# A hybrid attention step on one core: the instruction order from a simulated timeline

## The chip, the cores and the metric

The kernel runs on one core of a Trainium2 chip. The metric is device time in microseconds for one execution; several executions are timed and their median is taken. One further execution is run under the hardware profiler, and the profile lines below come from it.

## The reference, cut to what matters

One layer of a streaming encoder is computed for 1024 new frames of a prompt and for 8 running streams of 16 frames each with 1024 past frames. The input projection (2048 x 8192) yields queries, keys, values and gates of two head groups; the stick-breaking heads and the retention heads are computed; an output projection (2048 x 2048) follows. Everything is float32.

```python
p = jnp.einsum('btd,de->bte', rms_norm(x), w_in)          # q,k,v,gate of 8 stick-breaking + 8 retention heads
# stick-breaking: strictly causal, no softmax
z = einsum(q, k) * HEAD_DIM ** -0.5
log_keep = where(strict, log_sigmoid(-z), 0.0)
later = cumsum(log_keep, reverse=True) - log_keep
a = where(strict, exp(log_sigmoid(z) + later), 0.0);  o_sb = einsum(a, v)
# retention: chunks with a decaying state
o_r = einsum(einsum(q, k) * intra, v) + einsum(q, s) * decay_read
s = s * exp(lg * n) + einsum(k, decay_write, v)
y = concat(head_rms_norm(o_sb) * silu(gate_sb), head_rms_norm(o_r) * silu(gate_r))
x = x + rms_norm(einsum('bte,ed->btd', y, w_out))
```

## The kernel before, in words

The frames are cut into nine tiles of 128 rows: eight of the prompt (0 to 7) and one that holds the 8 streams x 16 frames (`SAMPLE`). They are worked in two groups. The first has tiles 0 to 3 and the sample tile (640 columns, in pieces of 256 and 384), the second tiles 4 to 7 (512 columns). For each group the normalized input stands in SBUF as a high and a low part (`mov`), and the kernel goes through eight heads. A head has six projections written as `project` (L206, 128 x 128 weights moving over the group's columns) and, for every two heads, two written as `project_rows` (L252, for the values). Every float32 product is three matmuls of high and low parts. Weights come through `load_w`: a load on SP's queue (L192), a high part by ScalarE (`split`, L127) and a low part by VectorE (L128), in four buffers each; a buffer holds four 128 x 128 blocks.

The attention itself is done in side jobs. A job is a Python generator; `project` and `project_rows` call `tick()` after each small set of matmuls, and a tick lets one due job trace its next step. A job's `yield n` says after how many ticks its next step is due (the `D_...` constants). This fixes the program order, in which the steps of the jobs lie between the matmuls of the projections. The jobs of a head are:

- `retention` with `ret_branch`: a transpose of the keys through HBM (`s_rk`, read back into `ro`, transposed by VectorE at L765), scores (L668), products into the bank `pa` (L686), new state (L701).
- `stick_breaking` with `sb_branch`: scores `z` (L535), sigmoids, a scan, a transpose of the weights through HBM (`s_be`), the last step of the transpose on VectorE (L525), products into `pa` (L559), copied out (L562).
- `decode`, in the first group: cached keys `kc` are loaded by POOL (L585), transposed by VectorE into `kcT` (L610), multiplied (L601); after the scan and a round trip through HBM (`s_bd`, L635) the weights multiply the cached values `vc` (loaded at L616, used at L648); the result is copied from `pa` at L654 and L656. Its first instruction is `qp` (L569).
- `finish`: head normalization, a transpose through HBM (`s_o`), the product with the gate, a store to `s_y`.

The bank `pa` exists once, the score bank `z` three times, the projection's accumulators twice. After the second group's last head the output projection runs in panels of 512 columns (`out_panel`, L879 and L889 to L891), for three groups of tiles.

Nothing in the text sets the order on an engine beyond this program order. Leaving the `TileContext` runs a list scheduler: it keeps the program order as priority, simulates the machine, and at each simulated moment gives an engine the ready instruction of the highest priority; buffers are given out in the same pass. The order in which it does this is the order of each engine's instruction list. Semaphore waits are then put in; on the chip every engine works through its list in order. In the kernel before, the simulation charges each instruction one duration.

## Time and profile before

| what | value |
|---|---|
| median of 3 runs | 2477.28 us (2473.57 to 2478.8) |
| profiled execution | 2463.17 us, of which the span from the first to the last instruction is 2461.1 us |
| granted TensorE clock | 0.988 |
| busy: TensorE, VectorE, ScalarE, POOL | 2367.9, 1250.0, 903.8, 641.9 us |
| DMA | 418.65 MB, mean 170 GB/s |

PE is TensorE's matmuls, PEld its weight loads, DVE VectorE, ACT ScalarE; SPq and the like are an engine's own queue of instructions such as DMA issues. A line of waits reads: engine, tile and line, what it waited for, the total us, how many times, the longest.

### The profile page before, as it was taken

How to read it: one execution, taken by the hardware profiler on the slowest of the kernel's cores; microseconds unless marked ns; L12 is line 12 of the kernel's file. 1: busy time of each engine (PE TensorE's matmuls, PEld its weight loads, DVE VectorE, ACT ScalarE, POOL GpSimd, SP SyncE). 2: the span in 40 equal slices, each digit the busy share in tenths (PEclk: the TensorE clock that was granted, in tenths of full speed). 3: DMA queues.
4: the chain of work that ended last, by engine and by line, in shares of the span. 5: the costliest groups of instructions: out<-in, count | busy, mean ns of one | idle time of the engine just before them, and what ended most of it. 6: DMA issues, size and time to landing. Idle time of an engine off the chain costs nothing.

```text
span 2461.1 us, 40322 instructions
## 1 busy us (share of the span) xinstructions
PE 2367.9 (96%) x14832; PEld 2099.4 (85%) x14832; DVE 1250.0 (51%) x2362; ACT 903.8 (37%) x1913; POOL 641.9 (26%) x1029
## 2 busy tenths in 40 slices
PE   7999899999999999998799999999999998999998
PEld 7999888989898888988578898889889886878787
DVE  8245454454444454444545544554564555564544
ACT  6323232333233232233334434344344443444333
POOL 3244354443433344333402111120220211000000
PEclk9999999999999999999999999999999998999999
DMA  7769677695948678495955655665564566665553
GB/s 241 165 144 210 143 191 173 173 199 140 212 125 221 149 177 178 130 226 146 209 161 150 153 152 142 144 163 135 153 160 128 152 152 170 224 221 191 184 184 133
DMA packets 673094, 418.65 MB, mean 170 GB/s; under 512 B 223744, under 2 KB 617984, under 8 KB 670464
## 3 DMA queue, kind: packets, MB, share of 16 engines
q1 hardware_dynamic: 523760, 285.99, 45.9%
q0 software_dynamic: 32256, 71.36, 12.5%
q10 hardware_dynamic: 116880, 58.74, 8.6%
q8 instruction: 116, 1.90, 0.3%
q14 instruction: 82, 0.67, 0.1%
HBM read 336.24 MB, written 79.69 MB: 169 GB/s over the span
## 4 chain that ended last, share of the span: by engine, by line
PE 75%; DMA 10%; issue 9%; DVE 4%; POOL 1%; ACT 1%; SPq 0%; ACTq 0%; DVEq 0%; POOLq 0%
PE acc L206 38%; PE accn L252 14%; PE a L890 4%; PE a L891 4%; PE a L889 4%; PE pa L559 2%; DMA vc<-cache_sb_v 2%; PE z L535 2%; DMA wr<-w_in 1%; PE zc L601 1%; DMA ro<-s_rk 1%; DMA kc<-cache_sb_k 1%; DMA s_rk<-rk 1%; PE pa L648 1%; DMA s_be<-be 1%
## 5 line engine op out<-in xcount | busy, mean ns | idle before, releaser
L206 PE MATMUL acc<-ml,wh 128*128 128x256 f32 (+2 forms) x2304 | 677.0, 343 | 0.2 <-DVE ml L128 0.2
L206 PE MATMUL acc<-mh,wh 128*128 128x256 f32 (+2 forms) x2304 | 670.5, 341 | 6.5 <-ACT rv L262 3.8
L206 PE MATMUL acc<-mh,wl 128*128 128x256 f32 (+2 forms) x2304 | 669.9, 341 | 3.7 <-DVE wl L128 3.7
L128 DVE TENSOR_TENSOR wl<-wr,wh 128x512 fp32r<-128x512 f32 (+1 forms) x576 | 394.7, 691 | 503.5 <-ACT wh L127 498.5
L127 ACT ACTIVATE wh<-wr 128x512 fp32r<-128x512 f32 (+1 forms) x576 | 356.6, 625 | 730.4 <-PE acc L206 367.9
L206 PEld LDWEIGHTS acc<-mh,wh 128*128 128x128 f32 x2304 | 425.3, 189 | 51.3 <-issue 14.3
L206 PEld LDWEIGHTS acc<-mh,wl 128*128 128x128 f32 x2304 | 425.1, 189 | 47.6 <-issue 12.2
L206 PEld LDWEIGHTS acc<-ml,wh 128*128 128x128 f32 x2304 | 422.5, 190 | 40.3 <-issue 12.4
L585 POOL DMA_DIRECT2D kc<-cache_sb_k x512 | 331.4, 653 | 367.8 <-DVE kcT L610 167.5
L252 PE MATMUL accn<-whn,mh 128*128 128x256 f32 x1152 | 332.5, 289 | 0.0
L252 PE MATMUL accn<-wln,mh 128*128 128x256 f32 x1152 | 326.9, 284 | 3.8 <-DVE wln L128 3.8
L252 PE MATMUL accn<-whn,ml 128*128 128x256 f32 x1152 | 326.5, 284 | 0.0
L252 PEld LDWEIGHTS accn<-whn,mh 128*128 128x128 f32 x1152 | 221.2, 192 | 12.9 <-issue 10.8
L890 PE MATMUL a<-wl,mh 128*128 128x512 f32 (+1 forms) x576 | 221.2, 384 | 7.7 <-DVE wl L128 7.7
L252 PEld LDWEIGHTS accn<-wln,mh 128*128 128x128 f32 x1152 | 221.3, 192 | 7.0 <-DVE wln L128 5.5
L252 PEld LDWEIGHTS accn<-whn,ml 128*128 128x128 f32 x1152 | 221.0, 192 | 1.7 <-issue 1.7
L891 PE MATMUL a<-wh,ml 128*128 128x512 f32 (+1 forms) x576 | 220.5, 383 | 0.0
L889 PE MATMUL a<-wh,mh 128*128 128x512 f32 (+1 forms) x576 | 219.3, 383 | 1.0 <-DVE sg L279 0.6
L890 PEld LDWEIGHTS a<-wl,mh 128*128 128x128 f32 x576 | 109.3, 190 | 31.3 <-DVE wl L128 10.6
L127 ACT ACTIVATE whn<-wrn 128x512 fp32r<-128x512 f32 x128 | 79.8, 634 | 151.2 <-PE acc L206 39.8
L441 POOL DMA_DIRECT2D be<-s_be x128 | 94.1, 741 | 142.4 <-DMA s_be<-be 124.0
L128 DVE TENSOR_TENSOR wln<-wrn,whn 128x512 fp32r<-128x512 f32 x128 | 86.8, 687 | 83.4 <-ACT whn L127 82.8
(184 smaller groups left out, 2602.4 us busy)
## 6 DMA issues: line engine op xcount, KB each, us to landing
wr<-w_in SPq DMA_DIRECT2D x384, 256.0 KB, 3.8
wr<-w_out SPq DMA_DIRECT2D x184, 256.0 KB, 3.6
wrn<-w_in SPq DMA_DIRECT2D x128, 256.0 KB, 3.1
kc<-cache_sb_k POOLq DMA_DIRECT2D x512, 64.0 KB, 4.3
vc<-cache_sb_v SPq DMA_DIRECT2D x64, 512.0 KB, 8.7
xt<-x_prompt SPq DMA_DIRECT2D x8, 1024.0 KB, 6.1
xr<-x_prompt SPq DMA_DIRECT2D x8, 1024.0 KB, 6.0
out<-out ACTq DMA_DIRECT2D x12, 512.0 KB, 2.9
```

Source lines behind the costliest of these rows:

```text
L127: nc.scalar.activation(hi, src, AF.Copy)
L128: nc.vector.tensor_tensor(lo, src, hi.bitcast(F32), ALU.subtract)
L206: last = nc.tensor.matmul(a[:, :m], lhs[:, j, :], rhs[w][:, j, o : o + m], start=(w == 0 and j == 0 and n == 0), stop=(w == KT // WQ - 1 a ...
L252: nc.tensor.matmul(a, lhs[q][:, jj, ts], rhs[:, j, :], start=(w == 0 and j == 0 and n == 0 and t % 2 == 0), stop=(w == KT // 2 - 1 and j = ...
L441: q.dma_start(raw[32 * i : 32 * i + 32, :].rearrange("p (k a) -> p k a", a=32), s[:, :, 32 * i : 32 * i + 32].rearrange("k (j b) a -> b (k ...
L535: nc.tensor.matmul(z[:, :c], q2[a][:, i * P : (i + 1) * P], k2[b][:, s : s + c], start=(m == 0), stop=(m == 2),)
L559: nc.tensor.matmul(po[:, :P], at[:, j, :], vn[:, j, :], start=(j == 0), stop=(j == t))
L585: nc.gpsimd.dma_start(kc[32 * i : 32 * i + 32, :].rearrange("p (k d) -> p k d", d=32), cache_k[0, 2 * c + j, s * 512 : (s + 1) * 512, h, 3 ...
L601: nc.tensor.matmul(z[r, :], qp[:, j, r], ready[c // 2][:, c % 2, :], start=(j == 0), stop=(j == 1))
L889: nc.tensor.matmul(a[:, :width], hi[q][:, j, ts], wh, start=(k == 0), stop=False)
L890: nc.tensor.matmul(a[:, :width], hi[q][:, j, ts], wl, start=False, stop=False)
L891: nc.tensor.matmul(a[:, :width], lo[q][:, j, ts], wh, start=False, stop=(k == KT - 1))
```

## The change

The context is told to build the order against a simulated timeline: instructions hold sequencers, queues and engines there, and transfers share the DMA engines, in place of one duration for each instruction. The kernel's text, its program order, its tiles and its buffers are the same.

```diff
-    with tile.TileContext(nc) as tc:
+    with tile.TileContext(nc, schedule_with_timeline_sim=True) as tc:
         tile_hybrid_step(tc, *args)
```

## Prediction

> **What bounds the kernel now.** I read the page first (busy shares and chain), then a table by stage, then TensorE's own waits, and then one stall instruction by instruction.
>
> ```profile
> span 2461.1 us, 40322 instructions
> PE 2367.9 (96%) x14832; PEld 2099.4 (85%) x14832; DVE 1250.0 (51%) x2362; ACT 903.8 (37%) x1913; POOL 641.9 (26%) x1029
> PE 75%; DMA 10%; issue 9%; DVE 4%; POOL 1%; ACT 1%; SPq 0%; ACTq 0%; DVEq 0%; POOLq 0%
> ```
>
> TensorE is busy for 2367.9 of 2461.1 us, so 93.2 us are idle in all, and that is nearly the most that a new order can give. The number of matmuls stays. The other engines have half their time free or more.
>
> ```profile
> core 0: us, PE busy (x) PEld busy (x) DVE busy (x) ACT busy (x) POOL busy (x), PEclk, DMA share, GB/s
> 0.00:42.00 42.00, 26.65 (x194) 25.70 (x195) 31.10 (x79) 26.95 (x44) 19.76 (x30) 0.96 0.83 274
> 42.00:1205.00 1163.00, 1123.83 (x8075) 1026.62 (x8075) 558.61 (x1132) 375.03 (x821) 454.11 (x757) 0.99 0.75 173
> 1205.00:1240.00 35.00, 25.80 (x187) 24.82 (x187) 17.97 (x25) 8.76 (x16) 6.92 (x11) 0.85 0.87 203
> 1240.00:1985.00 745.00, 744.18 (x4264) 648.28 (x4264) 392.46 (x687) 295.88 (x609) 126.37 (x196) 1.00 0.59 150
> 1985.00:2110.00 125.00, 112.12 (x511) 91.89 (x509) 67.10 (x123) 52.96 (x116) 18.34 (x28) 0.95 0.62 162
> 2110.00:2461.00 351.00, 335.31 (x1608) 282.11 (x1608) 182.80 (x319) 144.22 (x309) 16.44 (x7) 0.99 0.57 190
> ```
>
> These are the start, the eight heads of the first group (with the decode jobs), the hand-over between the groups, the second group, its end under the first output panel, and the output panels. The second group has 0.8 us of idle TensorE in 745: no order can better it, only spoil it. The first group has 39.2 us, the hand-over 9.2, the end 12.9. So what there is to win lies where side jobs run tightest. TensorE's waits say which:
>
> ```profile
> PE pa L559 <- DVE so L656: 12.2, 4, 7.5
> PE p0t L338 <- DVE dg L355: 10.5, 1, 10.5
> PE pa L559 <- DVE kp L525: 9.8, 4, 4.8
> PE pa L648 <- DMA vc<-cache_sb_v: 9.8, 5, 4.0
> PE a L890 <- DVE wl L128: 7.7, 7, 1.6
> PE rs L668 <- DVE rk L290: 5.1, 1, 5.1
> PE zc L601 <- DVE kcT L610: 3.9, 4, 1.6
> ...
> PE pa L641 <- DVE kp L635: 2.1, 2, 1.1
> ...
> PE zc L601 <- DVE kb L454: 1.0, 1, 1.0
> PE pSs L739 <- DVE st L742: 0.8, 1, 0.8
> ```
>
> (Total us, times, longest.) The small matmuls of the side jobs account for 12.2 + 9.8 + 9.8 + 5.1 + 3.9 + 2.1 + 1.0 + 0.8 = 44.7 us. The start (10.5) and the weights of the output panels (7.7) are apart. The longest, 7.5 us, shows what kind of fault it is. First two pieces of the chain of waits, then VectorE, then TensorE:
>
> ```profile
> 1092.49 7.66 DMA s_rk<-rk
> ...
> 1104.39 9.75 DMA ro<-s_rk
> ```
>
> ```profile
> 1107.07 0.71 DVE L610 STREAM_TRANSPOSE kcT<-kc 128x512 f32<-128x512 f32 x1 [5.05 <-DMA kc<-cache_sb_k]
> 1114.26 0.84 DVE L765 STREAM_TRANSPOSE rkn<-ro 128x640 f32<-128x640 f32 x1 [6.48 <-DMA ro<-s_rk]
> ...
> 1116.59 0.28 DVE L654 COPY so<-pa 128x128 f32<-128x128 f32 x1
> ...
> 1117.65 0.34 DVE L656 SCALAR_TENSOR_TENSOR so<-pa,dec,so 128x128 f32<-128x128 f32 x1
> ```
>
> ```profile
> 1118.14 1.62 PE L559 MATMUL pa<-vn,kb 128*128 128x128 f32 x6 [7.47 <-DVE so L656]
> ```
>
> VectorE stands at a transpose whose operand makes a round trip through HBM; the two transfers took 7.66 and 9.75 us. Behind it in the same queue stands the copy that would free the only `pa` bank, and TensorE waits for that bank. The list was built as if the round trip were shorter than it is.
>
> **The change, part by part.** No instruction is added or removed by the text. Priorities (program order), buffers and dependences stay; the simulated times at which something counts as ready differ, and with them the five engine lists and the queue of every DMA. Five things have a price.
>
> *Stalls that go.* Transfers that share engines and queue up come later in the simulated time, so what needs them is listed later. If that hits all the stalls above, 44.7 us go; if none, 0. I take all, since each waits on VectorE behind a transfer or on a transfer itself. The start (10.5) stays. TensorE also comes back slowly from a long stall:
>
> ```profile
> 1118.00:1121.00 3.00, 2.86 (x12) 2.89 (x13) 1.51 (x4) 0.40 (x2) 0.00 (x0) 0.50 0.56 159
> 1121.00:1125.00 4.00, 4.00 (x23) 4.00 (x22) 0.65 (x4) 2.19 (x6) 2.58 (x4) 0.68 0.24 66
> ```
>
> The clock is 0.50 and 0.68 after it: 3 x 0.50 + 4 x 0.32 = 2.8 us lost. With four waits of 4 us or more in the list (7.5, 5.1, 4.8, 4.0) that is 11 us beyond the 44.7, kept as the far end.
>
> *Small matmuls that come later.* This is the cost I expect. A queue in the simulated time can take the projection's matmuls as soon as their weights are split, well before TensorE gets to them; a side job's matmul that becomes ready then stands behind them. How much is ready ahead?
>
> ```profile
> ACT wh L127 <- PE acc L206: 367.9, 165, 8.2
> 42.07 15.88 PE acc L206 x99
> 1401.85 23.87 PE acc L206 x104
> ```
>
> ScalarE's split waits 165 times for TensorE to give back a weight buffer, so the four buffers are usually full. A buffer is 24 matmuls in the first group, at 15.88 / 99 = 0.160 us: 3.85 us; in the second it is 12 at 23.87 / 104 = 0.2295: 2.75 us. A side step can thus be late by one buffer at the least and three at the most; I take two, 7.7 us, the middle. The decode chain passes TensorE three times in series: scores (L601), first product with the values (L648), and the last, whose buffer the earlier ones free. That is 23.1 us per head. The slack at the end of a chain:
>
> ```profile
> 263.83 0.29 DVE L654 COPY so<-pa 128x128 f32<-128x128 f32 x1 [13.75 <-PE pa L648]
> ...
> 277.92 0.42 DVE L569 TENSOR_TENSOR qp<-qs,par 128x256 f32<-128x256 f32 x1
> L569 DVE TENSOR_TENSOR qp<-qs,par x8: 382/419/426, 130.6 to 1135.1; 128x256 f32<-128x256 f32 x8
> ```
>
> The first head's chain ends at 263.8 and the next begins at 277.9: 14.1 us. Before the last head it ends at 1116.6 (above) and the next begins at 1135.1: 18.5 us. The mean is 16.3. The excess, 23.1 - 16.3 = 6.8 us, comes at seven hand-overs: 47.6 us. With one buffer (11.6 us) there is no excess; with three (34.7 us) it is 7 x 18.4 = 129 us.
>
> *The last chain.* At 1985 to 2110 the last head's chain ends under the first panel with nothing after it to hide a delay. Two steps in series (scores, product) by two buffers of 2.75 us: 11 us; bounds 5.5 and 16.5.
>
> *Weights.* The loads on SP may be listed behind a transfer that waits.
>
> ```profile
> SPq L192 <- DVE wl L128: 505.8, 200, 6.9
> ...
> SPq L441 <- DMA s_bd<-be: 42.1, 8, 9.9
> ```
>
> SP mostly waits for a free buffer (505.8 us), so weights come early; the longest wait of a read-back is 9.9 us, and three full buffers cover 11.6. I cost this at nothing; the cover is gone when such a wait passes 11.6 us. For SP, and for POOL (26% busy), a gain at this place is excluded because TensorE hardly waits for weights in the two groups.
>
> *ScalarE's table loads.* Another order can change their number.
>
> ```profile
> L136 ACT ACT_TABLE_LOAD x27 | 34.6, 1283 | 3.6 <-DVE ov L135 3.1
> L459 ACT ACT_TABLE_LOAD x21 | 26.9, 1283 | 47.4 <-PE z L535 42.6 <-issue 3.8 <-DVE so L562 0.9
> ```
>
> Each is 1.28 us on an engine that is idle 63% of the time. I put it at 0; twice or half as many would be 62 us more or 31 less on ScalarE, hidden by the full weight buffers.
>
> Sum: -44.7 + 47.6 + 11 = +13.9 us. The profiled execution took 2463.17 us, 14.1 under the median of 2477.28 and below the lowest run; the difference is laid on the median: **2491.2 us**, with about 2477 for a profiled execution.
>
> **The rivals.**
>
> *Faster: the simulated queue is short.* Place: the same three steps in the first group. It decides at 16.3 / 3 = 5.4 us a step, which is 34 matmuls of 0.160 us. Below that the chains fit in their slack, the last chain costs 5.5, and 2477.28 - 44.7 + 5.5 = 2438 us; with half of the stalls gone 2460. For it: the 7.5 us stall is exactly a transfer taken as too short, and TensorE's other side-job waits look alike. Against it: full weight buffers stand ready ahead of nearly every side step. [...] No row here shows a depth.
>
> *No change.* The list on TensorE comes out nearly as it was, because priorities are the same and weights are early in both simulations: 2477, within 5 us. For it: 0.8 us of idle in the second group, where most matmuls already run unhindered. Against it: four other engines and the transfers are relisted as well.
>
> *Slower, by weights.* A read-back listed ahead of the weight loads waits twice as long as the longest now, 19.8 us, once in each of eight heads: 8 x (19.8 - 11.6) = 66 us, 2543. Against it: SP's slack above.
>
> **How the numbers follow.** A measurement of this kernel can tell about 0.2% (5 us) from no change. My forecast, chains late by more than the stalls give back, has 0.46; the short queue 0.40; no change 0.08; the weights 0.06. So faster 0.40, same 0.08, slower 0.52. The range runs from 2435, the short queue with every stall gone, to 2575, three buffers (-44.7 + 129 + 16.5 = +101, 2578); the clock's 11 us at the low end and the worse mixtures above are left out. It holds cases of both signs; the forecast's own range is 2483 to 2575.
>
> **What would show it.** In the new profile: L559, L648 and L601 stand with under 15 us in TensorE's waits (stalls gone); `so` L654 and the next `qp` L569 lie closer together or the head's period, 143.5 us (1135.1 - 130.6 over seven), grows by some 7 us (chains late); the second group keeps its 745 us; 1985:2110 grows by about 11. The forecast is wrong if the period shrinks, or if TensorE's waits for `wl` or `wh` grow past 30 us: then it is the weights.

## The result, and the profile after

The kernel with the new order takes 2500.35 us (median of 4 runs, 2496.96 to 2502.16), the kernel before 2477.32 us in the runs beside it: ratio 1.0094, 95% interval 1.0076 to 1.0111, so 23 us slower. The profiled execution took 2499.32 us, close to its median, while the profiled one of before lay 14 us under its own; the two traces therefore differ by 36.5 us of span, more than the medians do.

The head of the page of after, and its table by stage (us; then for TensorE, its weight loads, VectorE, ScalarE and POOL the busy us and instructions; clock; share of DMA; GB/s). The first two stretches have the limits that they had in the table of before; the later limits follow the same events.

```profile
span 2497.6 us, 40390 instructions
PE 2375.1 (95%) x14832; PEld 2102.7 (84%) x14832; DVE 1248.9 (50%) x2362; ACT 908.1 (36%) x1923; POOL 652.6 (26%) x1029
```

```profile
42.00:1205.00 1163.00, 1121.40 (x8101) 1029.30 (x8099) 562.58 (x1132) 371.87 (x821) 463.49 (x759) 0.98 0.76 174
1205.00:1240.00 35.00, 26.94 (x192) 24.94 (x193) 16.94 (x27) 10.81 (x19) 5.81 (x9) 0.85 0.80 196
1240.00:2006.00 766.00, 744.79 (x4248) 648.01 (x4247) 388.44 (x687) 299.81 (x614) 126.86 (x196) 1.00 0.56 144
2006.00:2134.00 128.00, 117.88 (x531) 96.51 (x531) 70.97 (x133) 56.44 (x126) 19.50 (x28) 0.95 0.62 173
2134.00:2497.60 363.60, 338.39 (x1580) 279.56 (x1578) 177.99 (x306) 141.59 (x302) 17.40 (x7) 0.97 0.55 179
```

In the 1163 us of the first group TensorE is idle for 41.6 us where it was idle for 39.2, and the last head of this group begins at 1133.6 us in place of 1135.1 (below): hardly a difference. The second group had 0.8 us of idle TensorE in 745 us; now it has 21.2 in 766, and that is the growth of this stage. The end under the first panel has 10.1 us of idle (12.9 before). The rest has grown from 351 to 363.6 us.

TensorE's own waits (total us, times, longest), the start's left out, and then the one wait that the second group had in before (1240 to 1985):

```profile
PE pa L641 <- DVE kb L454: 21.2, 7, 5.1
PE a L890 <- DVE wl L128: 14.8, 14, 7.5
...
PE pa L559 <- DVE kp L525: 11.9, 4, 5.6
PE accn L252 <- DVE wln L128: 8.7, 6, 2.6
PE acc L206 <- ACT vn L262: 6.6, 4, 3.1
PE pa L559 <- DVE kb L525: 6.3, 1, 6.3
PE pa L559 <- DVE kp L454: 5.4, 3, 2.6
PE pa L559 <- DVE so L656: 4.9, 4, 3.6
```

```profile
PE accn L252 <- DVE wln L128: 0.8, 3, 0.3
```

The old stalls at L648, L601 and L668 are gone and L656 is down from 12.2 to 4.9 us, but others stand in their place: 21.2 us at L641. In the second group the waits for the weights' low parts (`wln` L128) have grown from 0.8 to 8.7 us, and waits for the last step of a transpose (`kp` L525, 5.8 of its 11.9 us) and for `kp` L454 (5.4) are new. Why VectorE is late there shows in VectorE's waits on transfers in the second group, first of before (1240 to 1985), then of after (1240 to 2006):

```profile
DVE rk L504 <- DMA ro<-s_o: 4.4, 1, 4.4
DVE kp L525 <- DMA be<-s_be: 0.5, 2, 0.3
```

```profile
DVE kp L525 <- DMA be<-s_be: 57.8, 10, 9.3
DVE rk L504 <- DMA ro<-s_o: 33.8, 7, 8.6
DVE rkn L765 <- DMA ro<-s_rk: 28.3, 5, 8.4
DVE kT L504 <- DMA so<-s_o: 25.7, 7, 4.5
```

All are the transposes that close a round trip through HBM. The new list puts VectorE at them before the data is back: 3 times and 4.9 us became 29 times and 145.6 us. The transfers changed little in this group (medians of the 64 KB reads from issue to landing: `s_rk` 3.3 us in place of 3.4, `so` 2.4 in place of 2.3, `ro` from `s_o` 3.3 in place of 2.4), far less than the waits; so the place in the list is what I suspected, and the experiments test it. One case, VectorE and then TensorE (start, duration, instruction, and in brackets the wait ahead of it):

```profile
1450.57 0.71 DVE L765 STREAM_TRANSPOSE rkn<-ro 128x512 f32<-128x512 f32 x1 [8.36 <-DMA ro<-s_rk]
1451.32 0.49 DVE L769 TENSOR_SCALAR rkn<-rkn,dec 128x512 f32<-128x512 f32 x1
1451.72 0.69 DVE L128 TENSOR_TENSOR wln<-wrn,whn 128x512 fp32r<-128x512 f32 x1
```

```profile
1452.46 0.39 PE L252 MATMUL accn<-wln,mh 128*128 128x256 f32 x1 [2.64 <-DVE wln L128]
```

VectorE stands for 8.36 us, from 1442.2, with a weight split behind it in its queue. TensorE works on with the splits made ahead until 1449.8, and then waits the 2.64 us.

### The profile page after: what moved, and what is told of

The parts are those of the page before. It is cut to its first block, busy times and chain, and to the rows that moved or that the text cites. A ratio compares the mean times of both kernels' runs of the same rounds, so it can differ in the third digit from the quotient of the medians.

```text
span 2497.6 us, 40390 instructions
## 1 busy us (share of the span) xinstructions
PE 2375.1 (95%) x14832; PEld 2102.7 (84%) x14832; DVE 1248.9 (50%) x2362; ACT 908.1 (36%) x1923; POOL 652.6 (26%) x1029
## 4 chain that ended last, share of the span: by engine, by line
PE 49%; DMA 18%; issue 11%; DVE 5%; POOL 3%; ACT 3%; SPq 2%; ACTq 1%; DVEq 0%; POOLq 0%
PE acc L206 24%; PE accn L252 9%; DMA s_be<-be 4%; DMA mr<-s_y 3%; PE a L890 3%; PE a L891 3%; PE a L889 3%; DMA s_bd<-be 2%; POOL be L441 2%; DMA ro<-s_o 2%; SPq L441 1%; PE pa L559 1%; DMA be<-s_be 1%; DMA out<-kn 1%; DMA mr<-s_h 1%
## 5 line engine op out<-in xcount | busy, mean ns | idle before, releaser
L128 DVE TENSOR_TENSOR wl<-wr,wh 128x512 fp32r<-128x512 f32 (+1 forms) x576 | 388.3, 681 | 425.9 <-ACT wh L127 416.1
L206 PEld LDWEIGHTS acc<-ml,wh 128*128 128x128 f32 x2304 | 422.2, 190 | 43.6 <-issue 12.8
L252 PEld LDWEIGHTS accn<-whn,mh 128*128 128x128 f32 x1152 | 223.0, 194 | 16.3 <-issue 13.3
L889 PE MATMUL a<-wh,mh 128*128 128x512 f32 (+1 forms) x576 | 211.8, 387 | 5.3 <-ACT wh L127 4.4
L889 PEld LDWEIGHTS a<-wh,mh 128*128 128x128 f32 x576 | 108.8, 191 | 31.4 <-ACT wh L127 9.0
L128 DVE TENSOR_TENSOR wln<-wrn,whn 128x512 fp32r<-128x512 f32 x128 | 87.8, 688 | 84.0 <-ACT whn L127 83.7
```

The lines of the kernel that those rows point to most:

```text
L128: nc.vector.tensor_tensor(lo, src, hi.bitcast(F32), ALU.subtract)
L206: last = nc.tensor.matmul(a[:, :m], lhs[:, j, :], rhs[w][:, j, o : o + m], start=(w == 0 and j == 0 and n == 0), stop=(w == KT // WQ - 1 a ...
L252: nc.tensor.matmul(a, lhs[q][:, jj, ts], rhs[:, j, :], start=(w == 0 and j == 0 and n == 0 and t % 2 == 0), stop=(w == KT // 2 - 1 and j = ...
L889: nc.tensor.matmul(a[:, :width], hi[q][:, j, ts], wh, start=(k == 0), stop=False)
```

## The experiments

In the kernels below "held" means that an instruction is put behind all that was traced before it on its engine, in the list. Three theories stood after the comparison: R, read-backs listed too early stop VectorE; P, in the panels a burst of residual adds on VectorE stops the weight splits; M, the small matmuls of the side jobs come later on TensorE, as the prediction had it. Each ratio is to the kernel before in the runs beside it, with its 95% interval. In the lines of an edited kernel the line numbers are a few higher than in the kernel shown.

**The four read-back transposes held, under the new order and under the old.**

```diff
-                nc.vector.transpose(oT[:, :n], flat)
+                tc.keep_in_program_order(nc.vector.transpose(oT[:, :n], flat))
...
```

The edit at L525, L635 and L765 is the same.

> The changed kernel with the four transposes that read back from HBM (L504, L525, L635, L765) pinned on VectorE behind whatever was traced before them, so that the scheduler can't list them earlier than their program position. Theory R (the new order lists the consumers of read-backs too early; VectorE's waits on DMA rose from 175 to 334 us): VectorE's waits on DMA fall below 250 us, TensorE's waits in the second group (wln 8.7, kp L525 5.8, kp L454 5.4) fall to under half, and the time goes from 2500 to 2480-2490. Theory M of the prediction (small matmuls come later on TensorE): within 5 us of 2500. Theory P (a burst on VectorE in the output panels): second group falls not, 2500.

> The same four pins in the kernel before. R: the old order already lists these transposes later (L765 2.9 weight splits ahead of its program position, against 5.6 in the changed kernel), so the pin gives little: 2470-2482. If the pins themselves cost time (longer chains), it shows here: above 2485.

Under the new order: 2493.11 us, ratio to before 1.0071 (1.0053 to 1.0089), a little above the range expected of R. Under the old: 2479.11 us, 1.0029 (1.0012 to 1.0046). The gain under the new order is 7 us of 23, but by place it is clear: the seven periods of the second group (first L686 of its first head to that of its last) are 721.8 us before, 743.0 after, 722.7 with the transposes held, and VectorE's waits for transfers fell from 333.9 to 183.7 us. Under the old order the second group stays (720.7), while the first panel, under which the last head's jobs end, takes 71.2 us in place of 62.1: a held transpose has a price too. The first seven thousand projection matmuls were 1281.1 us in the profile of the new order with transposes held against 1266.0 in after's. I took that at first for a price of holding the transposes in the first group. One profile can't show it, since such a difference comes without any edit (below); but the medians speak for a price: with the transposes of the first group left free, the kernel took 11 us less (2482.02 us, below), and the two intervals do not meet.

**M: the projection's matmuls held.**

```diff
-                    last = nc.tensor.matmul(
+                    last = tc.keep_in_program_order(nc.tensor.matmul(
...
```

> The changed kernel with every matmul of the projections (L206) pinned behind what was traced before it on TensorE, so that a small matmul of a side job can't be overtaken by projections that are ready earlier. M: the second group and the first shrink, 2475-2490. R: TensorE now stands at small matmuls whose operand is late, 2505-2540.

2585.05 us, ratio 1.0448 (1.0415 to 1.0481). Taking the side jobs' matmuls at their place in the program makes TensorE wait at them, and the kernel loses 85 us more. Its waits from 42 to 1250 us (the end of the first group has moved to about 1290 us):

```profile
PE acc L206 <- ACT vn L262: 50.3, 4, 14.3
PE pa L648 <- DMA vc<-cache_sb_v: 43.3, 12, 6.1
PE pa L641 <- DVE kb L454: 20.7, 3, 7.1
```

So letting projections overtake small matmuls keeps TensorE busy in the first group. The second group, by itself, gained here: 733.2 us in place of 743.0, still above the 722.7 of the held transposes. This run alone does not say whether the new list has the small matmuls later than the old one. The order of the matmuls in the two traces does. For a decode job's first product with the cached values (L648), the projection matmuls ahead of it on TensorE are 1346, 2110, 2887, 3617, 4496, 5249, 6128 and 6816 in the eight heads before, and 1243, 1965, 2864, 3597, 4496, 5229, 6128 and 6816 after: never later, in five heads earlier. The decode scores (L601) are 6 earlier in the mean, and at most 15 later. In the second group the scores of the stick-breaking heads (L535) do come later, by 24 projection matmuls in the mean, but so they do in the run below in which only that group's transposes are held and the group takes 722.8 us. M falls on both counts.

**P: the residual adds of two of three row tiles (one before) moved from VectorE to ScalarE and POOL in the first two of the three groups of tiles that the panels go through**, under the new order and, as a control, under the old.

```diff
-                        store(n, rs[:, n : n + 1], slice(half * D // 2, (half + 1) * D // 2), n == m - 1)
+                        store(n, rs[:, n : n + 1], slice(half * D // 2, (half + 1) * D // 2), n >= 1)
```

> The changed kernel with two of three row tiles' residual additions of the output phase given to ScalarE and POOL (n >= 1 in place of n == m - 1), so that VectorE has two long L951 in a row and not four. P: the waits of L890 and L889 in the panels (13.0 and 2.9 us after 2134) fall to about half, 2490-2494. R and M: those waits come from elsewhere, 2500 within 4.

> Kernel before with the same move of residual adds, the control for e3. Theory P (the new list bunches four residual adds on VectorE ahead of the weight splits, which the old list does not): no gain here, 2477 within 4 us. Rival (the adds on VectorE cost panel time under either order): about 2467 us.

New order: 2490.40 us, 1.0065 (1.0042 to 1.0088), 10 us under after. Old order: 2483.59 us, 1.0028 (1.0012 to 1.0045), 8 us worse, which neither side of the expectation had; its panels grew from 415.0 to 422.2 us. Under the new order the panels, first to last of their matmuls, went only from 432.2 to 427.3 us, and their second quarter (432 of their 1728 matmuls; the expectations call it the second chunk), where the stall is, from 114.7 to 112.7. Where the other 5 us of the 10 come from, the profiles do not show. The old trace speaks against P: the same burst of four adds stands there, 7 us long, and TensorE waits 1.6 us at the most. VectorE in before, VectorE in after, and TensorE in after:

```profile
2185.58 7.02 DVE L951 SCALAR_TENSOR_TENSOR out<-out,out3r,xr 128x1024 f32<-128x1024 f32 x4
```

```profile
2217.28 9.05 DVE L951 SCALAR_TENSOR_TENSOR out<-out,out3r,xr 128x1024 f32<-128x1024 f32 x4
```

```profile
2226.99 0.79 PE L890 MATMUL a<-wl,mh 128*128 128x512 f32 x1 [7.49 <-DVE wl L128]
```

No weight split lies within either burst. In before one of the four adds takes 3.4 us in place of 1.3, in after two; each slow one runs beside an add of POOL's own (L949, 2.4 to 3.3 us long). So the edit is not a clean test of P: it takes adds off VectorE, but gives POOL four in place of two, and under the new order six weight splits beside those took 2.83 to 2.90 us in place of 0.69. What speaks against P is thus the old trace, and later the runs in which the burst stays and the stretch recovers.

The control gave something else as well. Its five engine lists are those of before up to the panels, yet its first seven thousand projection matmuls took 1283.3 us against 1268.6 in before's. A single profile's first group is not good to 15 us.

**The transposes held in the second group only; then with P's edit.**

```diff
+    def held(x):
+        return tc.keep_in_program_order(x) if phase[0] else x
...
-            nc.vector.transpose(kp[:, :n], be)
+            held(nc.vector.transpose(kp[:, :n], be))
...
```

The other three are edited likewise.

> Kernel after, with the four read-back transposes (L504, L525, L635, L765) held in program order in the second group only; the first group's side jobs are free as in the kernel after. Theory R (in the second group VectorE is parked at read-backs listed too early): the second group comes back from 743 to about 724 us, as when all groups were held, and the first group keeps its 1266 us for the first seven thousand projection matmuls; about 2500 - 19 = 2481 us. Rival (the held order helps the second group only because the first group, slowed by it, hands over with more done ahead): the second group stays at about 740 us and the time at 2495 to 2500.

> The kernel of e5 with the residual adds of two of three row tiles in the output panels on ScalarE and POOL instead of one of three. If the two effects (second group 19 us, panels 10 us) are separate places and add up: about 2500 - 19 - 10 = 2471 us, a little under the kernel before. If the 10 us came through a chance reordering of the list: about 2481 us, as e5.

2482.02 us, 1.0027 (1.0007 to 1.0046): 18 us under after, with a second group of 722.8 us. R holds there, and the rival, a handing-over of work by the first group, does not. With P's edit 2477.33 us, 1.0010 (0.9992 to 1.0027): a further 5 us gained, half of what adding up would give. VectorE's waits in the second group with the transposes held:

```profile
DVE kp L529 <- DMA be<-s_be: 30.3, 11, 8.5
DVE kT L508 <- DMA so<-s_o: 19.5, 7, 3.7
DVE rk L508 <- DMA ro<-s_o: 13.3, 7, 4.8
```

VectorE still waits 63 us in place of 146, and TensorE loses 5.6 us of these 752, in one wait for `kp`. So the waits that are left hardly reach TensorE.

**The panels again.** What differs between the lists ahead of the burst is ScalarE. Its largest waits in the 105 us before the burst in before, and in the 107 in after:

```profile
ACT mh L127 <- DMA mr<-s_y: 26.1, 16, 3.1
ACT wh L127 <- PE a L891: 15.1, 14, 1.5
```

```profile
ACT mh L127 <- DMA mr<-s_y: 55.8, 26, 4.2
...
ACT wh L127 <- PE a L891: 1.8, 1, 1.8
```

The next row tiles' operands (`mr`) are read from HBM scratch and split like the weights. The new list has ScalarE at them 26 times before they have landed, and it hardly ever gets so far ahead with weights that it waits for TensorE to free a buffer. Counted from the trace, the weight splits stand two to three steps (nine matmuls each) ahead of TensorE in the 5 us before the burst in the old order, and less than one in the new. This would be R again, on ScalarE. The test holds the high part of the operands' splits:

```diff
-            split(hi[q][:, j, at : at + n], lo[q][:, j, at : at + n], r)
+            h = hi[q][:, j, at : at + n]
+            cut = nc.scalar.activation(h, r, AF.Copy)
+            if panels[0]:
+                tc.keep_in_program_order(cut)
+            nc.vector.tensor_tensor(lo[q][:, j, at : at + n], r, h.bitcast(F32), ALU.subtract)
```

> Kernel after; in the output panels the first half of each split of the next row tiles' operands (mh, ScalarE, fed by a read of HBM scratch) is held behind what was traced before it on ScalarE. Theory R2 (the panels lose for the same reason as the second group: ScalarE is parked at mr reads listed too early, the weight splits lose their lead over TensorE, and the burst of four residual adds, which the old list has too, then is felt): ScalarE's wait for mr ahead of the second chunk falls from 55.8 to about 30 us, the second chunk from 114.7 to 101 to 105 us, the time from 2500 to about 2488. Rival (the burst itself is the cause): the second chunk stays at 112 to 115 us, 2500.

> Both repairs, the read-back transposes of the second group and the operand splits of the panels, in the kernel after. If the two places are all that the new list loses: 2482 - 12 = 2470 us, 0.2% under the kernel before. If the new list has no gain elsewhere (first group): about 2475 to 2478, the kernel before's time.

Alone: 2490.74 us, 1.0058 (1.0033 to 1.0083), 10 us under after, with ScalarE's wait for `mr` at 34.5 us and a second quarter of the panels of 103.9 us; the lead of the weight splits is two to three steps again. With the transposes of the second group held too: 2472.59 us, 0.9975 (0.9954 to 0.9997), the only version a little under the kernel before. The second quarter of its panels, ScalarE's waits in the 106 us ahead of the burst, and the burst, as long as in the old order:

```profile
2146.90:2251.80 104.90, 100.89 (x433) 82.21 (x434) 60.47 (x106) 48.20 (x108) 6.26 (x2) 0.98 0.62 195
```

```profile
ACT mh L191 <- DMA mr<-s_y: 33.6, 16, 4.1
ACT wh L127 <- PE a L900: 14.6, 12, 1.4
```

```profile
2184.72 7.04 DVE L960 SCALAR_TENSOR_TENSOR out<-out,out3r,xr 128x1024 f32<-128x1024 f32 x4
```

The burst is still there and the quarter is 10 us shorter, so the burst alone is not what cost the time.

**Both kernels profiled again, and the control of the last edit.**

> The kernel after unchanged, for a second profile of the same lists. What is due to the lists comes back: second group 743 us, panels 432 us with the stall at the burst. What is due to the single execution moves: the first group's first seven thousand projection matmuls, 1266.0 us in the first profile, should lie anywhere from 1265 to 1285 (two profiles with the old list for this part gave 1268.6 and 1283.4).

> The kernel before unchanged, for a second profile of it. Second group 721 to 722 us and panels 415 us come back if they belong to the lists; the first seven thousand projection matmuls move: 1268.6 us in its first profile, 1283.3 in another with the same lists; if its median of 2475 to 2477 is the usual execution, about 1280 us is expected here, and the new order's first group (1266.1 and 1279.5) is then no slower than the old one's.

> The kernel before with the operand splits of the panels held as in e8 and e9: the control for that repair. If only the new list had these splits too early: the time stays at 2476 within 4 us and the panels at 415 within 3 us. If holding them helps under either order: panels under 410 us and 2470 us or less, and the lead of e9 over the kernel before is this edit alone.

After again 2502.06 us (1.0107, 1.0072 to 1.0142), before again 2473.89 us (0.9993, 0.9982 to 1.0005), and the old order with the operand splits held 2477.64 us (1.0007, 0.9989 to 1.0025). That edit does nothing for the old order: its panels take 417.3 us against 415. The starts of the decode jobs (L569, first and last after the shapes' durations) in after, after again and before again:

```profile
L569 DVE TENSOR_TENSOR qp<-qs,par x8: 382/424/426, 131.8 to 1133.6; 128x256 f32<-128x256 f32 x8
```

```profile
L569 DVE TENSOR_TENSOR qp<-qs,par x8: 380/424/426, 133.4 to 1149.1; 128x256 f32<-128x256 f32 x8
```

```profile
L569 DVE TENSOR_TENSOR qp<-qs,par x8: 381/418/426, 132.1 to 1150.7; 128x256 f32<-128x256 f32 x8
```

What belongs to the lists came back, and the first group moved:

| us | old order | new order |
|---|---|---|
| last head of the first group starts (L569) | 1135.1, 1149.7, 1150.7, 1148.5 | 1133.6, 1142.4, 1149.1, 1136.3, 1136.0, 1142.0, 1131.3 |
| second group, seven periods (L686) | 721.8, 721.7, 721.8, 721.8 | 743.0, 738.6, 737.9, 747.0 |
| panels, first to last matmul | 415.0, 415.3 | 432.2, 430.4 |
| from there to the end | 27.5, 27.5 | 25.5, 25.4 |

(The columns take in those experiments that edit only a later part, for a row that lies ahead of the edit.) By means: first group 7 us shorter, second 20 longer, panels 16 longer, tail 2 shorter, and the two short pieces between these stages 2 longer and 3 shorter: in sum 26 us, against 23 to 27 by the medians. The 7 us are not settled: their standard error is about 4.

## Why the prediction was right or wrong

The sign was right, and 2491.2 us was 9 us short of 2500.35, but both came from terms that did not happen: that was luck.

*What bounds the kernel.* The stall that I followed, a transpose on VectorE whose operand is on a round trip through HBM, is the fault that sets the result. I took it for a fault of the old list that the new one would mend. In all, VectorE waited 174.9 us for transfers before and 333.9 after.

*Stalls that go, -44.7.* Failed. Single rows went (L648, L601, L668) or shrank, but L559, L648 and L601 together still make 28.5 us, not under 15, and L641 adds 21.2. TensorE's waits at the side jobs' small matmuls, 44.7 us before, are 50.1 after; in the second profiles they are 56.2 and 54.5. Idle in the first group is 39.2 and 49.0 us in two profiles of the old order, 41.6 and 51.2 in two of the new, over the same 1163 us.

*Small matmuls that come later, +47.6.* Failed. The head's period is 143.1 us in after's first profile and 145.1 in the second; before, 143.5 and 145.5. There was no excess at the hand-overs. The cause that the term gave is absent: a step was to be two buffers late, which is 48 projection matmuls, but on the new list the decode products (L648) stand nowhere later than on the old one, and the scores (L601) at most 15 matmuls later. The slack was too small as well: from the end of the last copy of a decode chain (L654) to the next `qp` it is 19.0 us in the mean of seven hand-overs before, not the 16.3 of the two that I read, and 18.8 after. These two terms together gave +2.9; neither happened, and the two errors cancelled. (The first group measured 7 us shorter, not settled.)

*The second group, no term.* This is the step that the result hangs on. I read 0.8 us of idle as "no order can better it, only spoil it" and then priced the spoiling at nothing; it was 20 us.

*The last chain, +11.* Failed: idle in this stage went from 12.9 to 10.1 us, and the first quarter of the panels took 129.8 us before and 129.7 after.

*The panels, no term.* +16 us. I looked for a late weight only on SP's queue. The sign that I set, TensorE's waits for `wl` and `wh` past 30 us, is just met when `wln` is counted (25.1 us without it, 33.8 with it). But the loads were not what was late: ScalarE's waits for weights from HBM (`wr`, `wrn`) fell from 111.0 to 72.7 us. The weights also pass ScalarE and VectorE, and there they stand behind operands that have not landed (ScalarE waited 55.8 us for `mr` ahead of the burst, in place of 26.1). The rival "slower, by weights" was thus the nearest in kind: work listed ahead of the weights waits for a transfer. It had the wrong queue.

*Table loads, 0.* Nothing speaks against it, though no run tested it: there are 65 in place of 55, 10 x 1.28 = 13 us more over the whole kernel on an engine that is busy for 36% of the time.

*The rivals.* Short queue and no change did not come. The 0.40 for the short queue rested on an assumption: no run shows how deep the simulated queue is. What the runs showed in its place is that the lateness of small matmuls, which that depth would have sized, did not appear at all at the three steps.

Shown by the runs: the early read-backs cost the second group its 20 us (held there alone, it returns to 722.8) and early operand reads cost the second quarter of the panels about 10 of its 13 (held, 103.9 and 104.9 from 114.7). The panels as a whole come to 422 us with these held, 7 more than in the old order; what makes up these 7 was not tested. Argued only: why the simulated timeline puts the read-backs early; the natural reading, that it takes their transfers as shorter than the 7.66 and 9.75 us that the prediction shows, was not tested. What in the first group might be gained by the new order stays open.

## What to carry to other kernels

VectorE took its list in order here: it stood for 8.36 us at a read-back, with a weight split behind it. That a list made from simulated times is as good as the simulated time of its slowest transfers is my reading, which no run tested. Look in the trace for engines that stand at an operand from HBM with work for TensorE behind them, and count how many steps ahead that work is. The stage that lost most to the new order here, 20 us, was the one without idle time (0.8 us of 745), so give such a stage a price and not a nought. A second profile of the same kernel is worth more than a third reading of the first: here one stage moved by 15 us between executions of the same lists, and two others by under 1 in the old order.

## What the runs showed of the hardware that was not expected

Here a stall can cost more than its length, because TensorE comes back at a lower clock; that the prediction had read from a long stall (0.50 and 0.68 after 7.47 us). What was not expected is how little it takes. Before the 7.49 us stall of the panels, and after it:

```profile
2212.00:2219.20 7.20, 6.97 (x30) 5.47 (x30) 7.02 (x17) 5.33 (x15) 0.00 (x0) 1.00 0.51 156
2227.00:2230.00 3.00, 3.00 (x7) 2.42 (x8) 2.28 (x5) 0.46 (x1) 0.00 (x0) 0.50 0.97 334
2230.00:2234.00 4.00, 4.00 (x13) 3.08 (x13) 0.55 (x1) 0.94 (x2) 0.00 (x0) 0.63 0.94 264
2234.00:2240.00 6.00, 6.00 (x28) 4.96 (x27) 2.82 (x6) 2.57 (x5) 0.00 (x0) 1.00 0.62 200
```

The clock is at 0.50 and 0.63 for 7 us. The second quarter of the panels in before and in after:

```profile
2148.40:2249.80 101.40, 98.61 (x434) 80.97 (x433) 61.63 (x112) 49.87 (x115) 5.60 (x2) 1.00 0.66 209
```

```profile
2169.60:2284.30 114.70, 104.45 (x433) 82.53 (x433) 60.45 (x106) 48.29 (x108) 5.66 (x2) 0.96 0.56 181
```

Of the 13.3 us that it grew, 7.5 are idle time and 5.8 are slower matmuls. The length of the stall alone does not decide it: a stall of 3.27 us in the third quarter of after was followed by 0.50, the same stall at the same place in after's second profile by 1.00:

```profile
2363.50:2367.00 3.50, 3.09 (x7) 2.48 (x8) 2.17 (x4) 0.63 (x1) 0.00 (x0) 0.50 0.84 290
```

```profile
2372.50:2376.00 3.50, 3.06 (x13) 2.55 (x14) 2.19 (x4) 0.63 (x1) 0.00 (x0) 1.00 0.84 290
```

Shorter ones can do it too. Between 2052 and 2056.4 us in after TensorE waited twice, for 1.16 and 1.51 us:

```profile
2052.00:2055.40 3.40, 1.67 (x7) 0.72 (x5) 2.53 (x3) 2.78 (x6) 1.14 (x2) 1.00 0.70 140
2055.50:2058.80 3.30, 2.46 (x6) 1.98 (x7) 3.30 (x4) 1.75 (x4) 1.10 (x2) 0.50 0.47 143
```

In the clock records of the fourteen traces a stretch at 0.50 lasts 3.41 us or a whole multiple of it (3.41, 6.83 and 10.24 us in before and after). The start and the end of a run left out, the full clock fell 199 times, 192 of them after 3.41 us in which TensorE was idle for half or more. In before and after it was 21 of 23; ahead of the other two it was idle for 40 and 48%. Ahead of the fall at the 3.27 us stall it was 58%, ahead of the one at the two short waits 52%. This is counted from the traces, whose matmul ends are modelled; no run was made to test it, and why the stall of 3.27 us left the clock at 1.00 in the second profile is not shown.

The other surprise is what an add on POOL does to VectorE. Counted over the panels of all fourteen traces, a weight split (`wl`, 128x512) takes 0.69 us at the median. Of the 31 that ran beside a residual add on POOL (L949) for over 0.3 us, 30 took 1.39 to 2.90 us; no other took more than 0.78. In before these are two, of 2.46 and 2.47 us, beside POOL's adds at 2194.25 and 2328.24 us. What the two engines share is not tested here, but moving work to POOL did not leave VectorE free.
